# Output weight tiles split at steps 44 to 47, late output banks exchanged, and the last gate products in two parts, in a hybrid decoder layer

## The chip, the cores and the metric

The kernel runs on one core of a Trainium2 chip. The metric is the device time of one execution in microseconds. The core has the engines PE (TensorE, matrix products), DVE (VectorE), ACT (ScalarE), POOL (GpSimd) and SP (SyncE, which issues the transfers). Each works through its own queue in order and waits on semaphores for the others.

## The reference, cut to what matters

One layer on 1024 tokens of width 1024, in float32. A combined projection feeds two mixers: dilated sliding-window attention (8 heads of 64, three patterns) and a gated linear recurrence (4 heads of 128). Their outputs, put side by side, go through one output product, and a squared-relu feed-forward layer follows.

```python
proj = h @ w_in[layer]
q_a, k_a, v_a, q_h, f_h, i_h, g_h = jnp.split(proj, splits, axis=-1)
attn = dilated_mixture_attention(q_a..., k_a..., v_a..., slopes)
attn = rmsnorm(attn.reshape(B, S, ATTN_WIDTH), attn_out_norm[layer])
rec = hgrn2_recurrence(q_h, f_h, i_h, g_h, lower_bounds[layer], hgrn_out_norm[layer])
mixed = jnp.concatenate([attn, rec], axis=-1) @ w_out[layer]
x = x + rmsnorm(mixed, mix_post_norm[layer])
h = rmsnorm(x, mlp_pre_norm[layer])
ff = jnp.square(jax.nn.relu(h @ w_ff1[layer])) @ w_ff2[layer]
x = x + rmsnorm(ff, mlp_post_norm[layer])
```

## The kernel before

Each operand of a product is split into a high and a low part, and a product is three passes on PE (`three_pass`, L88 to L91: high·high, low·high, high·low). One such triple on a 128x512 tile is called a **unit** here. A weight tile is loaded into one of two raw buffers (`raw`, by SP), then `w_split` makes its high part on ACT (L85) and its low part on DVE (L86), and then issues the load of the next tile in the stream; since there are two raw buffers, a load waits until the tile two places ahead has been split. `w_get(i, 0)` splits up to and including tile i. The eight tiles of the output weight are `WO0` to `WO0 + 7` (here tile 0 to tile 7), and `WO_TAG` names where their two parts go: `None` is the common pool (`wh`, `wl`), and a pair of letters names kinds of slabs (then the tiles are called `woh`, `wol`).

Order is written out by hand: nothing reorders the instructions of an engine. After the recurrence heads (`hgrn_core`) come 64 attention steps, `s = 8 * head + i`, where `i` runs over `ITEMS`: D0 to D3 (near blocks), F0 and F1 (far keys), N0 and N1. In each step one item's scores are raised (an exponential on ACT, L886), transposed on PE (`turn`, tiles pt_D, pt_F, pt_N) and split to pth/ptl, ptFh/ptFl or ptNh/ptNl; items of the step before are weighed (`weigh`, tiles pov and pov_far), and scores of later items are looked at (`look`, tiles ps_D, ps_F, ps_N; their reads with the bias go to pd, pf, pn on DVE, L836). Between these PE is given units of other work from `queue`: `UNITS` says how many in each step, half of them before `weigh` and half at the step's end, and `fill` takes one. Until step 47 the units are projections of the next head pairs (`attn_proj`: aq, av, ak, whose results are qf, vf, kf); at step 47 the rest of them is drained, `values_turn` transposes the last value half vf (tile pvt), and from then on the units are those of `early_out`: for tokens 0 to 511 the half of the output product that takes the recurrence outputs (tiles 0 to 3, bank pwe, result esum on ACT, L1092). `row_turn(t, 0)` transposes those recurrence rows (pmt) and splits them into emt.

`hooks` names what else is done at a step between its two halves of units: splits of output weight tiles, loads, norms and transposes of mixed rows. After step 63 the output products are finished with tiles 4 to 7 (`late_out`, bank pwo). Accumulators are four kinds of banks, two of each: mm, s, t and pv. The feed-forward product follows.

Tile 0 is split in before by `values(1)` of the last pair (its unit 4, at about step 44); tiles 1 to 3 and 4 to 6 by hooks, tile 7 behind the last step.

Of the kernel before, what the change touches and what calls it, by code (L numbers as in the profile page):

```python
# [11 lines left out]
AF = mybir.ActivationFunctionType  # L12
ALU = mybir.AluOpType
# [24 lines left out]
def hymba_layer(ctx, tc, x, w_in, w_out, w_ff1, w_ff2, g_pre, lb_logits, g_mix, g_post,  # L38
                g_mlp, g_mlp_post, bias_tab, level_masks, ident_in, fold_in, out):
    nc = tc.nc  # L40
# [112 lines left out]
    for i in range(4 * HH, 4 * HH + 3 * (AH // 2)):  # L153
        stream.append((w_in[i], None))
    WO0 = len(stream)
    WO_TAG = (None, None, ("S", "S"), ("S", "BT"), ("S", "S"), ("S", "T"), ("T", "T"), ("T", "T"))

    def wo_dest(k, tags):
        return lambda: (slab(tags[0], f"woh{k}", F32R), slab(tags[1], f"wol{k}", F32R))
# [12 lines left out]
    def fill(ns, least=False):  # L172
        debt[0] += ns
        if least:
            debt[0] = max(debt[0], 1.0)
        while debt[0] > 0 and queue:
            try:
                cost = next(queue[0])
            except StopIteration:
                queue.pop(0)  # L180
                continue
            if cost is None:
                break
            debt[0] -= cost
        debt[0] = min(debt[0], 0.0)
# [267 lines left out]
    def hgrn_core(h, scale, after=None):  # L453
# [150 lines left out]
        if after is not None:  # L604
            after()
        fill(1500 * scale)
        if h == HH - 1:
            look(0, "N", 0)
        for n in range(NT):
            V.scalar_tensor_tensor(gate[:, n], pos[n // 4][:, n % 4], rs[:, n:n + 1], gate[:, n],  # L610
                                   op0=ALU.mult, op1=ALU.mult)
        nc.sync.dma_start(out=mix_dram[:, h * P:(h + 1) * P].rearrange("(n p) d -> p n d", p=P), in_=gate)


    halves = ((0, 64), (64, 128))
# [106 lines left out]
    def attn_proj(pr):  # L722
        stacks = [{}, {}]
        box = [None]
        while pr > 1 and not second_done[pr - 2]:
            yield None
        w = w_get(A0 + 3 * pr, 0)
        for hf in range(2):
            sl = slice(hf * 512, hf * 512 + 512)
            for n, cost in enumerate(proj_t(w, f"aq{pr}", hf, box)):  # L730
                if hf == 0 and n == 2 and turn_later:
                    values_turn()
                    cost += 450.0
                if hf == 0 and n == 4:
                    w_get(A0 + 3 * pr)
                yield cost
            if hf == 0:
                for i in range(2):
                    stacks[i]["q"] = slab("S", f"q{pr}_{i}", F32R)
            full = half(f"qf{pr}{hf}")  # L740
            V.scalar_tensor_tensor(full, box[0], 0.125, rrow[:, sl], op0=ALU.mult, op1=ALU.mult)
            lo = half(f"ql{pr}{hf}", F32R)
            for i, (a, b) in enumerate(halves):
                S.activation(stacks[i]["q"][a:b, sl], full[a:b], AF.Copy)  # L744
                G.tensor_tensor(out=lo[a:b], in0=full[a:b], in1=f32(stacks[i]["q"][a:b, sl]), op=ALU.subtract)  # L745
            nc.sync.dma_start(out=f32(stacks[0]["q"][64:128, sl]), in_=f32(lo[0:64]))
            nc.sync.dma_start(out=f32(stacks[1]["q"][0:64, sl]), in_=f32(lo[64:128]))
            yield 650.0
        wv = w_get(A0 + 3 * pr + 1, 0)
        vs = None  # L750

        def values(hf):
            for n, cost in enumerate(proj_t(wv, f"av{pr}", hf, box)):
                if n == 4:
                    w_get(A0 + 3 * pr + 1 + hf)
                yield cost
            full = half(f"vf{pr}{hf}")
            V.tensor_tensor(out=by_class(full), in0=in_blocks(box[0]),
                            in1=in_blocks(rrow[:, hf * 512:hf * 512 + 512]), op=ALU.mult)
            turn_later.append((pr, vs, full, hf))  # L760
            yield 650.0

        vs = slab("V8", f"v{pr}", F32R, (P, NT, 2, 2, 64))
        yield from values(0)
        while pr > 0 and not first_done[pr - 1]:
            yield None
        wk = w_get(A0 + 3 * pr + 2, 0)
        for i in range(2):
            stacks[i]["kh"] = slab("S", f"kh{pr}_{i}", F32R)
            stacks[i]["kl"] = slab("S", f"kl{pr}_{i}", F32R)  # L770
        pairs[pr] = (stacks, vs)
        for hf in range(2):
            for n, cost in enumerate(proj_t(wk, f"ak{pr}", hf, box)):
                if n == 2 and hf == 0:
                    values_turn()
                    cost += 450.0
                yield cost
            keys_read(pr, box[0], hf)
            if hf == 0 and pr == AH // 2 - 1:
                early_rows()  # L780
            yield 650.0
        yield from values(1)
# [244 lines left out]
    def row_rec(t):  # L1027
        gain = gains["early"] if t < NE else gains["gmix"][:, :AW]
        G.tensor_tensor(out=rec_row(t), in0=rec_row(t), in1=gain, op=ALU.mult)

    def row_fin(t):
        return anats[-1][:, t].rearrange("p i d -> p (i d)")

    def row_norm(t):
        row = rows[t]
        dump = half(f"dm{t}")
        ss = col("ass", 2)
        sa = col("asa")
        ra = scales["row", t] = tp.tile([P, 1], F32, tag="era", name=f"era{t}") if t < NE else col("ara")
        S.activation(dump[:, :AL], row[:, AW:AW + AL], AF.Square, accum_out=ss[:, 0:1])  # L1040
        S.activation(dump[:, AL:AW], row_fin(t), AF.Square, accum_out=ss[:, 1:2])
        G.tensor_tensor(out=sa, in0=ss[:, 0:1], in1=ss[:, 1:2], op=ALU.add)
        rsqrt_mean(ra, sa, AW, 1)

# [151 lines left out]
    for h in range(HH):  # L1196
        last = h == HH - 1
        queue += [attn_proj(0), attn_proj(1)] if last else [hgrn_ig(h + 1), hgrn_qf(h + 1)]
        if last:
            S.activation(col("texp"), nhalf[:, :1], AF.Exp)  # L1200
        hgrn_core(h, 1.15 if last else 1.0, open_attention if last else None)
        if not last:
            drain()

    hooks = {
        45: lambda: row_rec(0),
        46: lambda: row_rec(1),
        47: lambda: row_turn(0, 0, tag="mm"),
        48: lambda: w_get(WO0 + 1, 0),
        49: lambda: [w_get(WO0 + 2, 0), load_bias(AH - 1), row_rec(2)],  # L1210
        50: lambda: [row_turn(1, 0), row_rec(3)],
        51: lambda: w_get(WO0 + 3, 0),
        52: lambda: [row_turn(2, 0), load_gain("gmix", "R", g_mix)],
        55: lambda: [row_load(t) for t in range(3)],
        59: lambda: [row_norm(0), row_gain(0)],
        60: lambda: [row_norm(1), row_gain(1)],
        61: lambda: [row_turn(0, 1, tag="s"), w_get(WO0 + 4, 0)],
        62: lambda: w_get(WO0 + 5, 0),
        63: lambda: w_get(WO0 + 6, 0),
    }  # L1220
    UNITS = ((2, 3, 3, 4, 3, 3, 3, 3), (3, 3, 3, 4, 2, 3, 3, 2), (3, 3, 3, 4, 2, 3, 3, 2), (2,) * 8)
    ITEMS = (("D", 0), ("D", 1), ("D", 2), ("D", 3), ("F", 0), ("F", 1), ("N", 0), ("N", 1))
    LOOKS = {0: ((0, "D", 2), (0, "N", 1)), 1: ((0, "D", 3), (0, "F", 0)), 2: ((0, "F", 1),),
             6: ((1, "D", 0),), 7: ((1, "D", 1),)}
# [3 lines left out]
    for s in range(n_steps):  # L1228
# [20 lines left out]
            far_queries(hd)  # L1249
        if kind != "D" or g % 2:  # L1250
            to_weigh.append((hd, kind, g // 2 if kind == "D" else g))
        units = UNITS[s // 16][i]
        for _ in range(units // 2):
            fill(0.0, True)
        to_fold, last_fold = [(*w, r) for w in ready for r in [weigh(*w)] if r is not None], to_fold
# [23 lines left out]
            swap_max(hd, int(i == 3))  # L1279
        if i == 7:  # L1280
            look(hd + 1, "N", 0)
        if s == 54:
            row_turn(3, 0, tag="s")
    for *w, r in to_fold:
        finish(*w, *r)
# [905 lines left out]
```

## Time and profile before

| | before |
|---|---|
| median of 3 runs | 1228.99 us (1228.61 to 1230.24) |
| profiled execution | 1228.77 us |
| its span in the trace | 1226.8 us |
| mean granted clock of PE | 0.993 |
| busy: PE, DVE, ACT, POOL | 98%, 71%, 45%, 26% |

In the listings of single instructions each row has its start, its duration, the engine, the line, the operation, the tile written and the tiles read, and the shapes; a bracket at the end gives the idle time of the engine just before it and what ended that. Attention runs from about 304 to 534 us of the span.

### The profile page before, as it was taken

How to read it: one execution, taken by the hardware profiler on the slowest of the kernel's cores; microseconds unless marked ns; L12 is line 12 of the kernel's file. 1: busy time of each engine (PE TensorE's matmuls, PEld its weight loads, DVE VectorE, ACT ScalarE, POOL GpSimd, SP SyncE). 2: the span in 40 equal slices, each digit the busy share in tenths (PEclk: the TensorE clock that was granted, in tenths of full speed). 3: DMA queues.
4: the chain of work that ended last, by engine and by line, in shares of the span. 5: the costliest groups of instructions: out<-in, count | busy, mean ns of one | idle time of the engine just before them, and what ended most of it. 6: DMA issues, size and time to landing. Idle time of an engine off the chain costs nothing.

```text
span 1226.8 us, 17215 instructions
## 1 busy us (share of the span) xinstructions
PE 1205.5 (98%) x6350; PEld 1032.1 (84%) x6350; DVE 868.7 (71%) x1478; ACT 547.4 (45%) x1067; POOL 322.8 (26%) x321
## 2 busy tenths in 40 slices
PE   9999999999999997999999999999999999999998
PEld 8898989888888886878888888888888888888886
DVE  5697979787676666568679667676678555488796
ACT  7633333222665665665575122222244354534562
POOL 0110111012222222145250676756622000000022
PEclk9999999999999998899999999999999999999999
DMA  5231413123453636163324446554487634433337
GB/s 216 70 91 57 120 57 107 35 81 99 120 130 91 162 101 165 54 208 134 135 106 161 167 170 223 202 183 155 156 317 270 234 103 155 154 103 88 118 103 274
DMA packets 86483, 174.21 MB, mean 142 GB/s; under 512 B 12160, under 2 KB 38784, under 8 KB 86400
## 3 DMA queue, kind: packets, MB, share of 16 engines
q1 hardware_dynamic: 86400, 173.12, 43.2%
q8 instruction: 50, 0.82, 0.3%
q14 instruction: 33, 0.27, 0.1%
HBM read 117.76 MB, written 49.04 MB: 136 GB/s over the span
## 4 chain that ended last, share of the span: by engine, by line
PE 94%; DVE 2%; ACT 2%; issue 1%; DMA 1%; SPq 0%; POOL 0%; DVEq 0%; POOLq 0%; ACTq 0%
PE f L1931 18%; PE f2s L1931 7%; PE pig L91 2%; PE pig L89 2%; PE pig L90 2%; PE pl L480 2%; PE pwo L89 2%; PE pwo L91 2%; PE pwo L90 2%; PE pm_f L89 1%; PE pm_f L91 1%; PE pm_f L90 1%; PE pm_ak L89 1%; PE pm_aq L89 1%; PE pm_aq L91 1%; PE pm_aq L90 1%
## 5 line engine op out<-in xcount | busy, mean ns | idle before, releaser
L86 DVE TENSOR_TENSOR al<-ar,ah 128x1024 fp32r<-128x1024 f32 x56 | 70.6, 1261 | 80.1 <-ACT ah L85 77.8
L1931 PE MATMUL f<-bh,ah 128*128 128x512 f32 x320 | 124.5, 389 | 0.0
L1931 PE MATMUL f<-bl,ah 128*128 128x512 f32 x320 | 124.5, 389 | 0.0
L1931 PE MATMUL f<-bh,al 128*128 128x512 f32 x320 | 124.5, 389 | 0.0
L85 ACT ACTIVATE ah<-ar 128x1024 fp32r<-128x1024 f32 x56 | 59.1, 1055 | 86.5 <-DMA ar<-actd 86.1
L1931 PEld LDWEIGHTS f<-bh,ah 128*128 128x128 f32 x320 | 60.1, 188 | 12.6
L1931 PEld LDWEIGHTS f<-bh,al 128*128 128x128 f32 x320 | 60.1, 188 | 12.5
L1931 PEld LDWEIGHTS f<-bl,ah 128*128 128x128 f32 x320 | 60.1, 188 | 12.3
L2005 POOL TENSOR_SCALAR lbl<-ssq 128x1 f32<-128x1 f32 x4 | 3.3, 821 | 245.6 <-ACT fd L2001 245.4
L1554 POOL TENSOR_TENSOR e<-x,e 128x512 f32<-128x512 f32 x14 | 21.6, 1541 | 131.1 <-DVE x L1505 123.9
L1931 PE MATMUL f2s<-bl,ah 128*128 128x512 f32 (+1 forms) x128 | 48.9, 382 | 0.0
L1931 PE MATMUL f2s<-bh,al 128*128 128x512 f32 (+1 forms) x128 | 48.9, 382 | 0.0
L1931 PE MATMUL f2s<-bh,ah 128*128 128x512 f32 (+1 forms) x128 | 48.9, 382 | 0.0
L985 POOL TENSOR_TENSOR anat<-anat,stat 128x128 f32<-128x128 f32 (+1 forms) x24 | 12.2, 509 | 115.8 <-DVE anat L984 105.2
L86 DVE TENSOR_TENSOR bl<-br,bh 128x1024 fp32r<-128x1024 f32 x32 | 40.1, 1253 | 1.2 <-ACT bh L85 1.1
L665 POOL COPY tout<-traw 128x256 f32<-128x256 f32 x16 | 11.9, 745 | 107.1 <-DMA traw<-in_bias_tab_dram 76.4
L1948 ACT ACTIVATE acc<-f 128x512 f32<-128x512 f32 x28 | 16.8, 598 | 49.7 <-PE f L1931 49.7
L86 DVE TENSOR_TENSOR wl<-raw,wh 128x1024 fp32r<-128x1024 f32 x23 | 30.0, 1306 | 10.7 <-ACT wh L85 10.7
L85 ACT ACTIVATE bh<-br 128x1024 fp32r<-128x1024 f32 x32 | 33.6, 1050 | 4.3 <-PE f L1931 2.9
L89 PE MATMUL pwo<-woh,mt 128*128 128x512 f32 x80 | 31.6, 395 | 1.3 <-ACT esum L1092 1.3
L701 POOL TENSOR_TENSOR kl<-kf,kh 64x512 fp32r<-64x512 f32 x16 | 22.2, 1390 | 39.7 <-ACT kh L700 37.4
L745 POOL TENSOR_TENSOR ql<-qf,q 64x512 fp32r<-64x512 f32 x16 | 21.4, 1338 | 42.3 <-ACT q L744 41.7
(1702 smaller groups left out, 4034.7 us busy)
## 6 DMA issues: line engine op xcount, KB each, us to landing
ar<-actd SPq DMA_DIRECT2D x56, 512.0 KB, 3.6
br<-in_w_ff_dram SPq DMA_DIRECT2D x16, 1024.0 KB, 6.2
w1r<-in_w_ff_dram SPq DMA_DIRECT2D x14, 1024.0 KB, 6.4
raw<-in_w_in_dram SPq DMA_DIRECT2D x26, 512.0 KB, 3.8
actd<-e SPq DMA_DIRECT2D x17, 768.0 KB, 4.3
actd<-e SPq DMA_DIRECT2D x11, 1024.0 KB, 4.1
vd<-v SPq DMA_DIRECT2D x16, 256.0 KB, 3.8
raw<-in_w_out_dram SPq DMA_DIRECT2D x8, 512.0 KB, 3.7
```

The lines of the kernel that those rows point to most:

```text
L85: S.activation(hi, src, AF.Copy)
L86: eng.tensor_tensor(out=lo, in0=src, in1=f32(hi), op=ALU.subtract)
L89: TE.matmul(dst, lhs[0], rhs[0], start=start, stop=False)
L90: TE.matmul(dst, lhs[0], rhs[1], start=False, stop=False)
L91: TE.matmul(dst, lhs[1], rhs[0], start=False, stop=stop)
L480: TE.matmul(pl[:, n % 2, :192], kt[:, n * P:(n + 1) * P], sets[u // 2][:, n % 4], start=True, stop=True)
L701: G.tensor_tensor(out=kl[a:b], in0=src, in1=f32(kh[a:b]), op=ALU.subtract)
L745: G.tensor_tensor(out=lo[a:b], in0=full[a:b], in1=f32(stacks[i]["q"][a:b, sl]), op=ALU.subtract)
L985: G.tensor_tensor(out=dst, in0=dst, in1=st["rd"][:, b].unsqueeze(2).to_broadcast([P, n, 64]), op=ALU.mult)
L1554: eng[0].tensor_tensor(out=e1[:, 3], in0=a21, in1=e1[:, 2], op=ALU.add)
L1931: TE.matmul(pm, a[:, j, c], b[:, j, d], start=start and j == 0 and q == 0, stop=stop and j == 1 and q == 2, skip_group_check=True)
L1948: S.activation(acc_at(p, i), pm, AF.Copy)
```

## The change

1. Tile 0 is split by the hook of step 44, tile 1 at 45 (it was 48), tile 2 at 46 (49), tile 3 at 47 (51), and tile 4 at 58 (61); tiles 5 to 7 stay. The places of tiles 1, 2 and 3 are exchanged.
2. Row products, row transposes, bias and row loads around these hooks move by one to four steps; `row_turn(0, 0)` uses a bank t in place of mm. `row_norm` is cut into two parts.
3. `late_out` takes a bank mm for odd and s for even row tiles (it was the other way round).
4. The last head's eight gate products, with the transfer that follows, leave `hgrn_core` and stand in the hooks of steps 0 and 1, four in each.
5. `values_turn` stands one unit later in aq and ak.
6. `UNITS` has a row for each head in place of one for two; heads 4 and 5 get one and three units fewer, head 6 one more, head 7 two fewer. What is left is drained where the queue was drained before. The number of instructions on each engine is the same.

```diff
-    WO_TAG = (None, None, ("S", "S"), ("S", "BT"), ("S", "S"), ("S", "T"), ("T", "T"), ("T", "T"))
+    WO_TAG = (None, ("S", "S"), ("S", "BT"), None, ("S", "S"), ("S", "T"), ("T", "T"), ("T", "T"))
...
+        def gated(g4):
+            for n in range(g4 * 4, g4 * 4 + 4):
+                V.scalar_tensor_tensor(gate[:, n], pos[g4][:, n % 4], rs[:, n:n + 1], gate[:, n],
+                                       op0=ALU.mult, op1=ALU.mult)
+            if g4 == 1:
+                nc.sync.dma_start(out=mix_dram[:, h * P:(h + 1) * P].rearrange("(n p) d -> p n d", p=P), in_=gate)
         if h == HH - 1:
             look(0, "N", 0)
-        for n in range(NT):
-            V.scalar_tensor_tensor(gate[:, n], pos[n // 4][:, n % 4], rs[:, n:n + 1], gate[:, n],
-                                   op0=ALU.mult, op1=ALU.mult)
-        nc.sync.dma_start(out=mix_dram[:, h * P:(h + 1) * P].rearrange("(n p) d -> p n d", p=P), in_=gate)
+            return gated
+        for g4 in range(2):
+            gated(g4)
...
-                if hf == 0 and n == 2 and turn_later:
+                if hf == 0 and n == 3 and turn_later:
                     values_turn()
...
-                if n == 2 and hf == 0:
+                if n == 3 and hf == 0:
                     values_turn()
...
-    def row_norm(t):
+    def row_norm(t, which=(0, 1)):
...
-        pm = pmo[t, hf] = bank("s" if t % 2 else "mm", f"pwo{t}_{hf}")
+        pm = pmo[t, hf] = bank("mm" if t % 2 else "s", f"pwo{t}_{hf}")
...
     hooks = {
-        45: lambda: row_rec(0),
-        46: lambda: row_rec(1),
-        47: lambda: row_turn(0, 0, tag="mm"),
-        48: lambda: w_get(WO0 + 1, 0),
-        49: lambda: [w_get(WO0 + 2, 0), load_bias(AH - 1), row_rec(2)],
-        50: lambda: [row_turn(1, 0), row_rec(3)],
-        51: lambda: w_get(WO0 + 3, 0),
-        52: lambda: [row_turn(2, 0), load_gain("gmix", "R", g_mix)],
-        55: lambda: [row_load(t) for t in range(3)],
-        59: lambda: [row_norm(0), row_gain(0)],
-        60: lambda: [row_norm(1), row_gain(1)],
-        61: lambda: [row_turn(0, 1, tag="s"), w_get(WO0 + 4, 0)],
+        0: lambda: last_gate(0),
+        1: lambda: last_gate(1),
+        43: lambda: row_rec(0),
+        44: lambda: [row_rec(1), w_get(WO0, 0)],
+        45: lambda: w_get(WO0 + 1, 0),
+        46: lambda: [row_turn(0, 0), w_get(WO0 + 2, 0)],
+        47: lambda: [w_get(WO0 + 3, 0), row_rec(2)],
+        49: lambda: [row_turn(1, 0), load_bias(AH - 1), row_rec(3)],
+        51: lambda: row_turn(2, 0),
+        52: lambda: load_gain("gmix", "R", g_mix),
+        55: lambda: [row_load(t) for t in range(2)],
+        57: lambda: [row_norm(t, (0,)) for t in range(2)],
+        58: lambda: w_get(WO0 + 4, 0),
+        59: lambda: [row_norm(0, (1,)), row_gain(0), row_load(2)],
+        60: lambda: [row_norm(1, (1,)), row_gain(1)],
+        61: lambda: row_turn(0, 1, tag="t"),
         62: lambda: w_get(WO0 + 5, 0),
         63: lambda: w_get(WO0 + 6, 0),
     }
-    UNITS = ((2, 3, 3, 4, 3, 3, 3, 3), (3, 3, 3, 4, 2, 3, 3, 2), (3, 3, 3, 4, 2, 3, 3, 2), (2,) * 8)
+    UNITS = ((2, 3, 3, 4, 3, 3, 3, 3), (2, 3, 3, 4, 3, 3, 3, 3), (3, 3, 3, 4, 2, 3, 3, 2), (3, 3, 3, 4, 2, 3, 3, 2),
+             (3, 3, 3, 3, 2, 3, 3, 2), (3, 3, 3, 3, 2, 2, 2, 2), (3, 2, 2, 3, 2, 2, 2, 1), (2, 2, 2, 3, 1, 2, 2, 1))
...
-        units = UNITS[s // 16][i]
+        units = UNITS[hd][i]
...
-        if s == 54:
+        if s == 53:
             row_turn(3, 0, tag="s")
```

How instructions stand on an engine then is shown at three places (line, operation, tile written, tiles read; numbers tell buffers apart). DVE around steps 44 to 47 in before, from the split of F0's far weights to those of N0; `vf` is the last value half, `ISA` the read of scores with the bias:

```order
L921 TENSOR_TENSOR ptFl_4927<-pt_F_4961,ptFh_4926 128x256
L923 TENSOR_TENSOR ptFh_4926<-pt_F_4961,ptFh_4926 64x128 x2
L984 TENSOR_REDUCE anat_4591<-pov_1_4947 128x2x64
L758 TENSOR_TENSOR vf_4991<-pm_av_4899,rrow 128x512
L836 ISA pd_4995,stat_4994<-ps_D_4997,bt_4683 128x128
L836 ISA stat_4994 128x1
L839 TENSOR_SCALAR stat_4994<-stat_4994 128x1
L926 TENSOR_TENSOR ptNl_5004<-pt_N_5002,ptNh_5003 128x4x128
```

The same stretch of DVE in after; `wol` and `emt` are low parts of tiles 1 and 2 and of the first recurrence rows:

```order
L927 TENSOR_TENSOR ptFl_4922<-pt_F_4957,ptFh_4921 128x256
L929 TENSOR_TENSOR ptFh_4921<-pt_F_4957,ptFh_4921 64x128 x2
L990 TENSOR_REDUCE anat_4588<-pov_1_4936 128x2x64
L86 TENSOR_TENSOR wol_4984<-raw_4624,woh_4983 128x1024
L842 ISA pd_4994,stat_4993<-ps_D_4996,bt_4680 128x128
L842 ISA stat_4993 128x1
L845 TENSOR_SCALAR stat_4993<-stat_4993 128x1
L932 TENSOR_TENSOR ptNl_5003<-pt_N_5001,ptNh_5002 128x4x128
L86 TENSOR_TENSOR emt_4794<-pmt_0_5025,emt_4794 128x512
L86 TENSOR_TENSOR wol_5033<-raw_4951,woh_5032 128x1024
L764 TENSOR_TENSOR vf_5041<-pm_av_4908,rrow 128x512
```

Two low halves of weight tiles and the one of emt have come ahead of `vf`.

ACT in before from the last key copy `kh_1` to the first hooks of step 48, where `wh_5115` is tile 1 and `v` the copy of pvt:

```order
L700 ACTIVATE kh_1_4673<-kf_4885 64x4x128
L886 ACTIVATE pd_4995,stat_4994<-pd_4995,stat_4994 128x128
L925 ACTIVATE ptNh_5003<-pt_N_5030 128x4x128
L713 ACTIVATE v_4568<-pvt_5041 128x8x64
L85 ACTIVATE emt_4778<-pmt_0_5062 128x512
L886 ACTIVATE pf_4996,stat_4994<-pf_4996,stat_4994 128x256
L925 ACTIVATE pth_0_5089<-pt_D_5088 128x128
L845 ACTIVATE qc_5094<-q_0_4431 128x512
L966 ACTIVATE pn_4749<-pov_far 128x512
L85 ACTIVATE wh_5115<-raw_4606 128x1024
```

ACT in after from the second copy of N0 to the split of tile 3 (`wh_5081`); `woh_5032` is tile 2:

```order
L931 ACTIVATE ptNh_5002<-pt_N_5001 128x4x128
L892 ACTIVATE pn_4746,stat_4682<-pn_4746,stat_4682 128x256
L706 ACTIVATE kh_1_4673<-kf_4897 64x4x128
L85 ACTIVATE emt_4794<-pmt_0_5025 128x512
L85 ACTIVATE woh_5032<-raw_4951 128x1024
L892 ACTIVATE pd_4994,stat_4993<-pd_4994,stat_4993 128x128
L931 ACTIVATE ptNh_5002<-pt_N_5049 128x4x128
L719 ACTIVATE v_4568<-pvt_5060 128x8x64
L85 ACTIVATE wh_5081<-raw_4987 128x1024
```

The copy of emt and the split of tile 2 now stand ahead of the last ptNh and of `v`, and that of tile 3 ahead of the next raise.

PE in before at the end of attention, from the units around the last transposes pt_N (step 63):

```order
L905 MATMUL pt_N_5645<-ident,pn_5375 128x128 x4
L89 MATMUL pwe_1_5567<-woh_5155,emt_4779 128x512
L90 MATMUL pwe_1_5567<-wol_5156,emt_4779 128x512
L91 MATMUL pwe_1_5567<-woh_5155,emt_4779 128x512
L960 MATMUL pov_far<-ptNh_5617,v_4568 128x4x32
L960 MATMUL pov_far<-ptNl_5618,v_4568 128x4x32
L960 MATMUL pov_far<-ptNh_5617,v_4568 128x4x64
L960 MATMUL pov_far<-ptNl_5618,v_4568 128x4x64
L89 MATMUL pwe_0_5566<-woh_5220,emt_4779 128x512
L90 MATMUL pwe_0_5566<-wol_5221,emt_4779 128x512
L91 MATMUL pwe_0_5566<-woh_5220,emt_4779 128x512
L89 MATMUL pwe_1_5567<-woh_5220,emt_4779 128x512
```

PE in after at the same place:

```order
L89 MATMUL pwe_1_5521<-wh_5081,emt_4795 128x512
L90 MATMUL pwe_1_5521<-wl_5082,emt_4795 128x512
L91 MATMUL pwe_1_5521<-wh_5081,emt_4795 128x512
L911 MATMUL pt_N_5658<-ident,pn_5385 128x128 x4
L966 MATMUL pov_far<-ptNh_5628,v_4568 128x4x32
L966 MATMUL pov_far<-ptNl_5629,v_4568 128x4x32
L966 MATMUL pov_far<-ptNh_5628,v_4568 128x4x64
L966 MATMUL pov_far<-ptNl_5629,v_4568 128x4x64
```

The units that stood between the last pt_N and pov_far, and among the parts of pov_far, are gone from there: they come earlier.

More of the change, by code (lines that the diff above doesn't have):

```diff
@@ L1032, in row_fin @@
         return anats[-1][:, t].rearrange("p i d -> p (i d)")
-    def row_norm(t):
+    def row_norm(t, which=(0, 1)):
         row = rows[t]
-        dump = half(f"dm{t}")
-        ss = col("ass", 2)
+        if 0 in which:
+            ss = scales["part", t] = col("ass", 2)
+            S.activation(half(f"dm{t}")[:, :AL], row[:, AW:AW + AL], AF.Square, accum_out=ss[:, 0:1])
+        if 1 not in which:
+            return
+        ss = scales.pop(("part", t))
         sa = col("asa")
         ra = scales["row", t] = tp.tile([P, 1], F32, tag="era", name=f"era{t}") if t < NE else col("ara")
-        S.activation(dump[:, :AL], row[:, AW:AW + AL], AF.Square, accum_out=ss[:, 0:1])
-        S.activation(dump[:, AL:AW], row_fin(t), AF.Square, accum_out=ss[:, 1:2])
+        S.activation(half(f"dn{t}")[:, AL:AW], row_fin(t), AF.Square, accum_out=ss[:, 1:2])
         G.tensor_tensor(out=sa, in0=ss[:, 0:1], in1=ss[:, 1:2], op=ALU.add)
@@ L1200, in hymba_layer @@
             S.activation(col("texp"), nhalf[:, :1], AF.Exp)
-        hgrn_core(h, 1.15 if last else 1.0, open_attention if last else None)
+        last_gate = hgrn_core(h, 1.15 if last else 1.0, open_attention if last else None)
         if not last:
```

## The prediction

> **What bounds the kernel now.** I read the page first, then what PE (TensorE) waits for, then stretches of the span, then single instructions.
>
> ```profile
> PE 1205.5 (98%) x6350; PEld 1032.1 (84%) x6350; DVE 868.7 (71%) x1478; ACT 547.4 (45%) x1067; POOL 322.8 (26%) x321
> PE 94%; DVE 2%; ACT 2%; issue 1%; DMA 1%; SPq 0%; POOL 0%; DVEq 0%; POOLq 0%; ACTq 0%
> ```
>
> PE is busy for 98% of the span and carries 94% of the chain that ended last. So only two things can move the time: gaps in PE's work, and PE running slow. All PE waits from the attention part on (engine, tile, line, what it waited for: us in total, times, longest):
>
> ```profile
> PE pwe L89 <- ACT woh L85: 3.3, 1, 3.3
> PE pwe L90 <- DVE wol L86: 2.2, 2, 1.6
> ...
> PE pwo L89 <- ACT esum L1092: 1.3, 1, 1.3
> PE pwe L89 <- ACT wh L85: 1.2, 1, 1.2
> PE ps_D L831 <- DVE stat L836: 1.1, 1, 1.1
> PE pwe L89 <- DVE v L714: 1.1, 1, 1.1
> PE pwe L90 <- DVE wl L86: 0.8, 1, 0.8
> ...
> PE pov_far L960 <- DVE ptNl L926: 0.6, 1, 0.6
> ...
> PE pvt L710 <- DVE vf L758: 0.4, 1, 0.4
> PE pt_F L908 <- ACT pf L886: 0.4, 1, 0.4
> PE pt_N L905 <- ACT pn L886: 0.3, 1, 0.3
> PE pwe L89 <- ACT esum L1092: 0.2, 1, 0.2
> ```
>
> The two at the beginning of attention, ps_D and pvt, are 1.5 us. The six of pwe and pov_far that name v, ptNl, wh, wl, woh and wol lie around steps 47 to 50: the early output products start there and their weight tiles are not split yet. The four that remain (pwo, pt_F, pt_N, and pwe for esum) are 2.2 us at the end of attention. By stretches (us, busy of PE, PEld, DVE, ACT, POOL, granted clock, DMA share, GB/s):
>
> ```profile
> 466.00:498.00 32.00, 22.99 (x109) 19.14 (x108) 17.18 (x53) 15.84 (x38) 7.29 (x7) 0.79 0.59 168
> 498.00:530.00 32.00, 31.20 (x200) 27.00 (x199) 19.80 (x64) 23.71 (x70) 6.51 (x14) 1.00 0.11 30
> 470.00:476.00 6.00, 4.08 (x25) 3.30 (x25) 3.90 (x14) 3.43 (x6) 0.00 (x0) 1.00 0.77 178
> 476.00:480.00 4.00, 4.00 (x18) 3.53 (x16) 1.97 (x10) 2.03 (x4) 0.00 (x0) 0.59 0.75 229
> 480.00:484.00 4.00, 2.38 (x14) 1.85 (x14) 2.49 (x7) 0.11 (x1) 3.08 (x3) 0.93 0.72 210
> 484.00:490.00 6.00, 3.54 (x17) 3.08 (x15) 2.44 (x8) 3.00 (x9) 0.92 (x1) 0.75 0.65 206
> 490.00:497.00 7.00, 5.61 (x19) 4.63 (x19) 3.16 (x9) 3.75 (x10) 0.40 (x1) 0.53 0.44 150
> ```
>
> From 466 to 498 PE is idle for 32.00 − 22.99 = 9.0 us, and its clock is 0.79; in the next 32 us the clock is 1.00. All idle that matters: 1.5 + 9.0 + 2.2 = 12.7 us. The clock costs more on top: 4 × 0.41 + 4 × 0.07 + 6 × 0.25 + 7 × 0.47 = 6.7 us, of which 0.47 × (7.00 − 5.61) = 0.6 fell on idle, so 6.1. Single instructions show both (start, us, and in brackets the idle before it):
>
> ```profile
> 475.60 0.49 PE L90 MATMUL pwe<-wl,emt 128*128 128x512 f32 x1 [0.75 <-DVE wl L86]
> 482.02 0.50 PE L90 MATMUL pwe<-wol,emt 128*128 128x512 f32 x1 [1.61 <-DVE wol L86]
> 490.84 0.79 PE L89 MATMUL pwe<-woh,emt 128*128 128x512 f32 x1 [3.29 <-ACT woh L85]
> 494.02 0.78 PE L89 MATMUL pwe<-woh,emt 128*128 128x512 f32 x1
> 495.45 0.41 PE L942 MATMUL pov<-pth,v 128*128 128x256 f32 x1
> 529.26 0.39 PE L89 MATMUL pwe<-woh,emt 128*128 128x512 f32 x1
> 529.96 0.39 PE L89 MATMUL pwe<-woh,emt 128*128 128x512 f32 x1
> ```
>
> A product of three passes (a unit) takes 529.96 − 529.26 = 0.70 us at full clock and 495.45 − 494.02 = 1.43 us behind the stalls. Before loses 12.7 + 6.1 = 18.8 us that the change could reach.
>
> **The change part by part.** The rows that carry prices:
>
> ```profile
> 307.04 2.15 DVE L610 SCALAR_TENSOR_TENSOR gate<-po,hrs,gate 128x128 f32<-128x128 f32 x8
> 309.11 0.54 DVE L836 CUSTOM_DVE_ANT_0 pd<-ps_D,bt 128x384 f32<-128x384 f32 x1
> 464.66 1.10 DVE L758 TENSOR_TENSOR vf<-pm_av,rrow 128x512 f32<-128x512 f32 x1
> 467.27 0.60 PE L710 MATMUL pvt<-ident,vf 128*128 128x128 f32 x4
> 462.76 0.35 SPq L106 DMA_DIRECT2D raw<-in_w_out_dram  x1
> 473.24 1.05 ACT L85 ACTIVATE wh<-raw 128x1024 fp32r<-128x1024 f32 x1
> 474.32 1.22 DVE L86 TENSOR_TENSOR wl<-raw,wh 128x1024 fp32r<-128x1024 f32 x1
> 528.62 0.59 ACT L925 ACTIVATE ptNh<-pt_N 128x512 fp32r<-128x512 f32 x1
> 530.00 0.33 SPq L106 DMA_DIRECT2D raw<-in_w_out_dram  x1
> 533.60 1.07 ACT L85 ACTIVATE woh<-raw 128x1024 fp32r<-128x1024 f32 x1
> 534.71 1.22 DVE L86 TENSOR_TENSOR wol<-raw,woh 128x1024 fp32r<-128x1024 f32 x1 [1.19 <-ACT woh L85]
> 536.10 0.40 PE L90 MATMUL pwo<-wol,mt 128*128 128x512 f32 x1
> ```
>
> *Last gate products in two parts.* Eight products hold DVE for 2.15 us ahead of the score read pd at 309.11, for which ps_D waits 1.1. In hooks 0 and 1 four (1.07) stand behind that read, where PE has units to do. The 1.1 goes; pvt, one unit (0.70) later, loses its 0.4. Gain 1.5; if the halves delayed a later read it would be 0.4. The mixd transfer goes out a step later; SP's order is unchanged and the early rows are read 40 steps on.
>
> *Weight splits at steps 44 to 47.* These take away the late tiles: the waits for wh, wl, woh and wol, the one for v (pmt now takes a bank t, so pwe need not wait until pvt was read) and with them most of 9.0 us. What is late next is read off the queues. On DVE, vf (the last value tile, from which pvt is made) now stands behind wol of tile 2. That tile's load can go out only when tile 0's low half has freed its buffer: 462.76 before, up to 0.7 earlier now, since the new table puts two units fewer ahead of step 44. A load takes 533.60 − 530.00 = 3.6, so the tile is there at 465.7 to 466.4. Then 1.05 on ACT, 1.22 on DVE, and 1.10 of vf: it ends at 469.1 to 469.8, in place of 465.8. PE comes to pvt at 466.7 (467.27 less the wait of 0.6) to 467.3. The new wait of pvt is therefore 1.8 to 3.1 us; I take 2.65, since ACT has an emt copy just ahead. Behind it DVE splits tile 3 ahead of the reads of pn: of its 1.22 I leave 0.75 as a wait of ps_N, the rest lying beside PE's pwe unit, and 0.25 for pt_N at steps 46 and 47, behind two ACT splits. Sum 3.65 (2 to 6), in place of 9.0.
>
> *Tile 4 at step 58.* Its low half (1.22 on DVE) stands ahead of the joint maximum of the far scores, and the raise and pt_F follow from that. Before, pt_F waited 0.4 there with no split. Below: 0.4, all hidden. Above: 1.05 + 1.22 = 2.3. I take 1.45 as the whole loss there, nearer to the DVE price.
>
> *The end.* The pwo bank exchange takes away the wait for esum, 1.3. But the last tile's chain stays: its load goes out at 530.00 when tile 5's low half is done, and runs through ACT (533.60) and DVE (534.71) to the product at 536.10, 6.1 us. Before, PE did 6.1 − 1.3 = 4.8 of work meanwhile. The new table moves three units (2.1) from there to earlier steps, and with tile 4's split (1.05 on ACT) gone from step 61 the chain can start that much sooner: 4.8 − 2.1 + 1.05 = 3.75 of work, 2.35 lost; 3.4 if ACT is no earlier. Where PE meets it: no unit stands between the last pt_N and its pov_far now, where three stood, so it waits for ptNh (0.59 on ACT, behind other ACT work; I take 1.05) and ptNl (0.75), and the last 1.45 for tile 7. I take the sum of these, 3.25 (2.35, or up to 4.15 where ptNl's wait comes on top of 3.4), nearer to the case without a sooner ACT, since the raises of N1 still stand there. It takes the place of 1.8 (pwo, pt_N, esum); pt_F's 0.4 is counted above.
>
> *At nothing.* Units moved between steps are the same count at 0.70; PE has as many instructions as before. The row products, norms and loads that move stand on POOL (26% busy by the page) and on ACT beside units. Without that cover a norm part, an ACT pass over at most 384 columns, would cost no more than ptNh's 0.59. The slabs exchanged hold tiles that are free by then. FF1's first bank now follows tile 7's pwo; a clash there would cost one DVE read of a bank, some 1.1 by the row of vf.
>
> *The clock.* Stalls after: 3.65 + 1.45 + 3.25 = 8.35. Is PE slowed again? In before, 1.2 + 0.8 of idle close together at 474 to 476 preceded 476:480 at 0.59, and the 1.3 at the end preceded nothing. The pvt wait of 2.65 is nearer to the first, so one such stretch, 4 × 0.41 = 1.6, and 0.4 for a second at the end: 2.0 (0 to 6.1). The Trainium skill, "TensorE: Matmul & The Clock Gate", section "Part 1: The HAM clock gate (the "warmup" mystery)", has half speed only after an idle window of about 3.4 us. The trace does not agree: 0.59 came with no single idle over 1.2. By that rule this term would be 0.
>
> Sum: losses 8.35 + 2.0 = 10.35 in place of 18.8, a gain of 8.45. Against the profiled execution's own 1228.77 us (span 1226.8 and 2.0 around it) that gives 1220.3. The median of the runs is 1228.99, 0.2 away, which I neglect.
>
> **The rivals.**
> *A, the backlog hides.* ACT and DVE catch up beside the units; losses of the three places fall to their lower ends, 2 + 0.4 + 2.35 = 4.75, no slow stretch. Gain 14.05: 1214.7. For it: DVE is idle for over 14 of the 32 us from 466. Against: the load of tile 2 can't be there earlier.
> *B, stalls as forecast but no slow stretch.* Gain 18.8 − 8.35 = 10.45: 1218.3. For it: the pwo wait of 1.3 left the clock at 1.00. Against: 476:480.
> *C, stalls as forecast and the clock drops as long as before.* Losses 8.35 + 6.1 = 14.45, gain 4.35: 1224.4. For it: three stalls over 1.5 us would do what 482.02 and 490.84 did.
> *D, slower: the softmax falls behind ACT.* Three splits at steps 45 to 47 stand ahead of raises and copies on ACT and of reads on DVE. Should each of steps 47 to 50 wait out one split of both, 1.05 + 1.22 = 2.27, that adds 9.1; with a clock loss of 6.1 the losses are 8.35 + 9.1 + 6.1 = 23.6, 4.8 more than before: 1233.6. It decides once losses pass 18.8, that is, from about two such steps with the full clock loss. Against: from 498 to 530 ACT is 23.71 of 32 busy and PE waited for next to nothing.
>
> **How the numbers follow.** A measurement of this kernel can tell about 0.2%, 2.5 us, from no change. Forecast 0.37, A 0.20, B 0.12, C 0.16, losses within 2.5 us of before's 0.05, D 0.10. Faster: 0.37 + 0.20 + 0.12 + 0.16 = 0.85; same 0.05; slower 0.10. The range reaches from 1213, where A's first place loses next to nothing too, to 1227, C with the upper ends of all three places (6 + 2.3 + 4.15 = 12.45 + 6.1 = 18.55 would be 1228.5; I take a good half of the way there); D and a fifth of A lie outside.
>
> **What would show it.** Right: no wait of pwe for wh, wl, woh or wol; a wait of pvt for vf of 1.8 to 3.1; some 1.4 of pt_F behind step 58; pov_far and pwo waiting for ptNh, ptNl and wol at the end; ps_D's 1.1 gone; one stretch of clock near 0.6. Wrong: pvt without a wait (A), clock below 0.8 over some 30 us (C), or raises late in every step from 47 to 50 (D).

## The result, and the profile after

The changed kernel takes 1220.01 us (median of 4 runs, 1219.55 to 1220.62) beside 1228.82 of the kernel before (4 runs, 1228.61 to 1230.24): a ratio of 0.9926, 95% interval 0.9909 to 0.9943. The profiled execution took 1219.76 us, its span is 1218.0 and the mean granted clock 0.997.

What PE waits for in the whole span of the kernel after:

```profile
PE pvt L716 <- DVE vf L764: 3.0, 1, 3.0
PE pt_F L914 <- ACT pf L892: 1.5, 2, 1.0
...
PE pwo L90 <- DVE wol L86: 0.8, 1, 0.8
PE pt_N L911 <- DVE ptNl L932: 0.7, 1, 0.7
PE pov_far L966 <- ACT ptNh L931: 0.6, 1, 0.6
PE ps_F L837 <- DVE stat L842: 0.6, 1, 0.6
...
PE pov_far L966 <- DVE ptNl L932: 0.5, 1, 0.5
PE pwo L89 <- ACT woh L85: 0.4, 1, 0.4
```

No product of the early output (pwe) waits for a split tile any more. In the place of those waits stands one wait of pvt, 3.0, with pt_N's 0.7 just ahead. The other rows are pt_F (1.5, behind step 58), four at the end (0.6 + 0.5 + 0.4 + 0.8 after rounding, 2.2 by single rows) and a new one, ps_F's 0.6 at step 1. The same 32 us as before, and the two stretches behind the wait of pvt (columns as in the prediction):

```profile
466.00:498.00 32.00, 28.65 (x180) 25.54 (x181) 22.45 (x69) 20.73 (x56) 4.96 (x6) 0.95 0.68 181
```

```profile
470.47:473.10 2.63, 2.63 (x10) 2.34 (x11) 1.73 (x5) 1.48 (x3) 0.00 (x0) 0.50 0.68 211
473.10:476.00 2.90, 2.90 (x21) 2.69 (x21) 2.77 (x10) 2.35 (x7) 0.00 (x0) 0.97 0.65 144
```

PE is idle for 32.00 − 28.65 = 3.4 us instead of 9.0, and the clock is 0.95 instead of 0.79. The clock is 0.50 for 2.63 us and then near full speed: 0.50 × 2.63 + 0.03 × 2.90 = 1.4 us lost in place of 6.1. The wait of pvt and what made it, on PE, DVE, POOL and ACT in turn:

```profile
470.47 1.11 PE L716 MATMUL pvt<-ident,vf 128*128 128x128 f32 x4 [3.04 <-DVE vf L764]
471.23 0.78 PE L89 MATMUL pwe<-wh,emt 128*128 128x512 f32 x1
472.66 0.41 PE L837 MATMUL ps_N<-kh,q 128*128 128x256 f32 x1
```

```profile
460.62 1.84 DVE L86 TENSOR_TENSOR wl<-raw,wh 128x1024 fp32r<-128x1024 f32 x1 [0.87 <-ACT wh L85]
464.04 1.22 DVE L86 TENSOR_TENSOR wol<-raw,woh 128x1024 fp32r<-128x1024 f32 x1
467.35 2.11 DVE L86 TENSOR_TENSOR wol<-raw,woh 128x1024 fp32r<-128x1024 f32 x1 [0.39 <-ACT woh L85]
469.38 1.03 DVE L764 TENSOR_TENSOR vf<-pm_av,rrow 128x512 f32<-128x512 f32 x1
```

```profile
458.83 2.54 POOL L1035 TENSOR_TENSOR erows<-erows,etable 128x512 f32<-128x512 f32 x2
464.08 1.43 POOL L991 TENSOR_TENSOR anat<-anat,stat 128x128 f32<-128x128 f32 x1 [2.71 <-DVE anat L990]
467.11 1.27 POOL L1035 TENSOR_TENSOR erows<-erows,etable 128x512 f32<-128x512 f32 x1
```

```profile
465.63 0.60 ACT L85 ACTIVATE emt<-pmt 128x512 fp32r<-128x512 f32 x1
466.25 1.06 ACT L85 ACTIVATE woh<-raw 128x1024 fp32r<-128x1024 f32 x1
```

vf runs right behind tile 2's low half, as the order said. But that half took 2.11 us where the prediction had 1.22. Tile 0's low half (460.62) was long too, 1.84, beside two POOL products; so it freed tile 2's buffer late, and the load went out at 462.48, 0.3 earlier than before where up to 0.7 was forecast. Behind the wait a unit of pwe takes 472.66 − 471.23 = 1.43 us, half speed, as in the stretches of before.

### The profile page after: what moved, and what is told of

The parts are those of the page before. It is cut to its first block, busy times and chain, and to the rows that moved or that the text cites. A ratio compares the mean times of both kernels' runs of the same rounds, so it can differ in the third digit from the quotient of the medians.

```text
span 1218.0 us, 17222 instructions
## 1 busy us (share of the span) xinstructions
PE 1200.7 (99%) x6350; PEld 1028.1 (84%) x6350; DVE 868.3 (71%) x1478; ACT 546.9 (45%) x1067; POOL 323.4 (27%) x321
## 4 chain that ended last, share of the span: by engine, by line
PE 94%; ACT 2%; DVE 2%; issue 1%; DMA 1%; SPq 0%; POOL 0%; DVEq 0%; POOLq 0%; ACTq 0%
PE f L1945 18%; PE f2s L1945 7%; PE pig L91 2%; PE pig L89 2%; PE pig L90 2%; PE pl L480 2%; PE pwo L90 2%; PE pwo L91 2%; PE pwo L89 2%; PE pm_f L89 1%; PE pm_ak L89 1%; PE pm_f L91 1%; PE pm_f L90 1%; PE pm_ak L91 1%; PE pm_ak L90 1%; PE pm_av L89 1%
```

## The experiments

Each ratio is to the kernel before, run on the same chip (its medians there were 1228.19, 1229.00 and 1228.87 us in the three groups of four); the changed kernel's is 0.9926. The intervals are about ±0.0016, that is ±2 us, and most of that is the spread of the kernel before (4 to 7 us in a group, against 0.6 to 2.7 for most of the others). Two kernels of the lists are therefore compared by their medians: differences under 1 us are not told apart, and between groups the medians of before themselves differ by up to 0.8.

### The early splits undone, and the early splits alone

```diff
-        44: lambda: [row_rec(1), w_get(WO0, 0)],
-        45: lambda: w_get(WO0 + 1, 0),
-        46: lambda: [row_turn(0, 0), w_get(WO0 + 2, 0)],
-        47: lambda: [w_get(WO0 + 3, 0), row_rec(2)],
+        44: lambda: row_rec(1),
+        46: lambda: row_turn(0, 0),
+        47: lambda: row_rec(2),
+        48: lambda: w_get(WO0 + 1, 0),
...
+        49: lambda: [w_get(WO0 + 2, 0), row_turn(1, 0), load_bias(AH - 1), row_rec(3)],
+        51: lambda: [w_get(WO0 + 3, 0), row_turn(2, 0)],
```

(and `WO_TAG` as before.)

> The changed kernel with one part undone: tiles 0 to 3 are split where they were before (tile 0 by the value units, 1 to 3 at steps 48, 49 and 51) and lie where they did. Theory of the prediction: the waits of pwe for split tiles (9.0 us) and the clock loss behind them (6.1) come back, and pvt's wait of 3.0, pt_N's 0.7 and their slow stretch (about 1.1) go, so +10 us: 1230. Rival, that the new table of units and not the earlier split took the waits away: under +4 us, 1220 to 1224.

Measured: 1224.25 us, 0.9963 (0.9949 to 0.9977), 4.2 slower than the changed kernel. The time is far from the theory's 1230 and just above the rival's range, but the rival's reason does not hold either: the waits come back, only smaller than they were.

```profile
PE pwe L90 <- DVE wol L86: 2.0, 2, 1.2
PE pwe L89 <- ACT woh L85: 1.7, 1, 1.7
...
PE pwe L89 <- ACT wh L85: 1.2, 1, 1.2
...
PE pwe L90 <- DVE wl L86: 0.8, 1, 0.8
...
PE pvt L716 <- DVE vf L764: 0.6, 1, 0.6
```

That is 2.0 + 1.7 + 1.2 + 0.8 + 0.6 = 6.3 us in place of 9.0 in before, and the clock from 466 to 498 is 0.89 in place of 0.79. At the end pov_far waits for nothing here, and pwo only 0.3 for wol, though the table of units is the new one.

The other way round, the kernel before with the splits moved and nothing else:

```diff
-        45: lambda: row_rec(0),
-        46: lambda: row_rec(1),
-        47: lambda: row_turn(0, 0, tag="mm"),
-        48: lambda: w_get(WO0 + 1, 0),
+        44: lambda: w_get(WO0, 0),
+        45: lambda: [row_rec(0), w_get(WO0 + 1, 0)],
+        46: lambda: [row_rec(1), w_get(WO0 + 2, 0)],
+        47: lambda: [row_turn(0, 0, tag="mm"), w_get(WO0 + 3, 0)],
```

> The kernel before with one part of the change alone: tiles 0 to 3 split at steps 44 to 47, at their new places; the table of units, the banks, tile 4 and the gate products are as before. Theory: the late tiles' waits and the clock loss behind them go; vf stands ahead of tile 2's low half with the old table, so pvt hardly waits; pwe still waits for v, about 1: 9 to 11 us faster than before, 1217 to 1219. Rival, from the run with late splits, which lost only 4 us: 4 to 5 faster, 1224.

Measured: 1219.65 us, 0.9929 (0.9917 to 0.9942): 9 us, as much as the whole change. Alone, the splits also bring waits with them (the profiled execution took 1221.42 us):

```profile
PE pwe L89 <- DVE v L714: 2.2, 1, 2.2
PE pov_far L960 <- DVE ptNl L926: 1.7, 2, 1.2
...
PE pwo L90 <- DVE wol L86: 0.8, 1, 0.8
```

pwe waits for v 2.2 us here (1.1 in before); pmt still stands in a bank mm, and v's low part comes late behind the splits, but no run parts the two. The end already has the waits of the changed kernel, though the table is the old one: pov_far waits 0.32 for ptNh and 0.50 for ptNl there (the other 1.16 of its 1.7 falls at 468.6), and pwo 0.76 for wol. And pwo does not wait for esum, though the banks are the old ones. So the splits are worth 9 us beside the old table and banks and 4 beside the new ones; the parts do not add up.

### Rows and banks alone, the table of units alone

Only `row_rec(0)`, `row_rec(1)` and `row_turn(0, 0)` moved (43, 44, 46; bank t):

> The kernel before with the first row products at 43 and 44 and the first row transpose at 46 in a bank t, nothing else. Theory: pwe's wait for v of 1.07 and pov_far's 0.56 go, and the tiles are as late as ever: PE meets them earlier, and 0 to 2 us are won, 1226 to 1228. Rival, that this part made the six us by which the run with late splits has less loss in the middle than before: 1222 to 1223.

Measured: 1227.31 us, 0.9989 (0.9980 to 0.9998): 1.4 us faster, as the theory said. v's wait is gone, and woh's is still 3.0.

Only `UNITS` new:

> The kernel before with the new table of units alone. Theory: the table costs where the splits are early, since it pushes vf behind tile 2's low half, but gains where they are late, since fewer units are asked for while the tiles are not split: the waits of pwe fall from 9.0 to about 6.5 and the clock loss with them, 3 to 6 us, 1223 to 1226. Rival, that it costs in both: 1229 to 1231.

Measured: 1227.80 us, 0.9990 (0.9977 to 1.0003): no difference that can be told, so both theories miss. Taken at their middle values, these two parts (1.4 and 1.2, the second not told apart from none) and the gate products (0.9 by their waits) make about 3.5 of the 4.6 us by which the kernel with late splits beats the kernel before. The rest of that is not attributed.

### The table of units undone

```diff
-        units = UNITS[hd][i]
+        units = UNITS[s // 16][i]
```

(with the old table.)

> The changed kernel with the table of units as before. Theory: three units stand at the end of attention again and cover 1.5 of its 2.2 us of waits, the pvt wait stays at about 3: -1 to -1.5 us, 1218.8. Rival, that the earlier splits need the fewer units of heads 4 and 5 ahead of them: the pvt wait grows by up to 1.4 and the time by 1 to 3 us, 1221 to 1223.

Measured: 1216.64 us, 0.9901 (0.9885 to 0.9916): 3.4 faster than the changed kernel, more than expected. Part of it is the end, where pov_far and pwo wait 1.2 in place of 2.2 and pt_F 1.1 in place of 1.5; the larger part is the middle:

```profile
PE pt_N L911 <- DVE ptNl L932: 2.0, 1, 2.0
...
PE pwe L89 <- DVE v L720: 0.7, 1, 0.7
```

```profile
466.00:498.00 32.00, 29.59 (x192) 26.09 (x193) 23.62 (x79) 23.39 (x61) 5.22 (x6) 1.00 0.68 181
```

pvt does not wait, since vf now stands ahead of tile 2's low half; pt_N waits 2.0 in its place, and the clock stays at 1.00. To see which rows of the table do it, those of heads 4 and 5 alone were put back:

```diff
-             (3, 3, 3, 3, 2, 3, 3, 2), (3, 3, 3, 3, 2, 2, 2, 2), (3, 2, 2, 3, 2, 2, 2, 1), (2, 2, 2, 3, 1, 2, 2, 1))
+             (3, 3, 3, 4, 2, 3, 3, 2), (3, 3, 3, 4, 2, 3, 3, 2), (3, 2, 2, 3, 2, 2, 2, 1), (2, 2, 2, 3, 1, 2, 2, 1))
```

> The changed kernel with the rows of heads 4 and 5 of the table as before, those of heads 6 and 7 new. Theory: the units missing ahead of step 44 made the value tile late, so the middle is that of the run with the old table (no wait of pvt over 1, clock 1.00) and the end that of the changed kernel (2.2 of waits): 2 to 2.5 us faster than the changed kernel, 1217.7. Rival, that heads 6 and 7 make the difference: 1219 to 1220.

Measured: 1217.68 us, 0.9902 (0.9884 to 0.9919), the time expected. In its trace the middle is that of the whole old table (pt_N 2.0, no wait of pvt, clock 1.00 from 468 to 476) and the end that of the changed kernel. On DVE, vf stands ahead of tile 2's low half:

```profile
464.70 1.06 DVE L764 TENSOR_TENSOR vf<-pm_av,rrow 128x512 f32<-128x512 f32 x1
467.52 2.13 DVE L86 TENSOR_TENSOR wol<-raw,woh 128x1024 fp32r<-128x1024 f32 x1 [0.16 <-ACT woh L85]
```

So the four units taken from heads 4 and 5 make vf late: the value product ends later against the hooks, which stay at their steps. (Head 7 gets one unit fewer by the new row, 15 in place of 16, not two as the list of the change says.)

### vf ahead of tile 2

```diff
-        46: lambda: [row_turn(0, 0), w_get(WO0 + 2, 0)],
-        47: lambda: [w_get(WO0 + 3, 0), row_rec(2)],
+        46: lambda: row_turn(0, 0),
+        47: lambda: [w_get(WO0 + 2, 0), row_rec(2)],
+        48: lambda: w_get(WO0 + 3, 0),
```

> The changed kernel with tile 2 split by the hook of step 47, behind the value transpose, and tile 3 by that of 48, so that vf no longer stands behind tile 2's low half on DVE. Theory: pvt's wait of 3.04 us goes, and the slow stretch behind it (about 1.3) with it: -3 to -4 us, 1216 to 1217. Rival, that DVE and ACT are simply full there: the wait reappears at pwe for wol or at ps_N, under -1.5 us.

Measured: 1216.04 us, 0.9896 (0.9883 to 0.9910), 4 faster than the changed kernel. The theory holds: pvt's wait falls to 0.58, the clock is 1.00, and no pwe waits for tile 2 or 3 though they are split a step later.

```profile
467.54 0.66 PE L716 MATMUL pvt<-ident,vf 128*128 128x128 f32 x4 [0.58 <-DVE vf L764]
```

```profile
466.00:498.00 32.00, 30.85 (x201) 27.27 (x201) 23.32 (x79) 22.83 (x61) 4.52 (x6) 1.00 0.65 179
```

PE has only 32.00 − 30.85 = 1.2 us of idle left there. A little of the rival shows all the same: ps_N waits 0.6, which it did not in the changed kernel.

### POOL's product moved away from the split

```diff
-        44: lambda: [row_rec(1), w_get(WO0, 0)],
+        44: lambda: [row_rec(1), row_rec(2), w_get(WO0, 0)],
...
-        47: lambda: [w_get(WO0 + 3, 0), row_rec(2)],
+        47: lambda: w_get(WO0 + 3, 0),
```

> The changed kernel with row_rec(2), a POOL product over erows, moved from the hook of step 47 to that of 44. In the changed kernel tile 2's low half took DVE 2.11 us in place of 1.22, while POOL worked on kl and erows. Theory, that POOL's work beside it is the cause: the low half takes 1.22 to 1.6, pvt's wait falls from 3.04 to 2.2 to 2.6, the time by 0.5 to 1.3 us. Rival, that it is the weight load that lands then: 2.11 stays and so does the time.

Measured: 1219.54 us, 0.9925 (0.9911 to 0.9938): the mechanism as expected, the time unchanged within what can be told. Tile 2's low half takes 1.23, and pvt's wait is 1.88, less even than the 2.2 to 2.6 expected. But the moved product now stands in the way of tile 0's low half, which took 1.84 beside two POOL products in the changed kernel and takes 3.08 beside three (DVE, POOL and PE in turn):

```profile
460.18 3.08 DVE L86 TENSOR_TENSOR wl<-raw,wh 128x1024 fp32r<-128x1024 f32 x1 [0.86 <-ACT wh L85]
467.89 1.23 DVE L86 TENSOR_TENSOR wol<-raw,woh 128x1024 fp32r<-128x1024 f32 x1 [0.22 <-ACT woh L85]
```

```profile
459.66 2.53 POOL L1035 TENSOR_TENSOR erows<-erows,etable 128x512 f32<-128x512 f32 x2
```

```profile
463.78 0.33 PE L960 MATMUL pov_far<-ptFl,vf 128*128 128x128 f32 x1 [0.55 <-DVE ptFl L927]
467.13 0.66 PE L911 MATMUL pt_N<-ident,pn 128*128 128x128 f32 x4 [0.97 <-DVE ptNl L932]
470.12 0.66 PE L716 MATMUL pvt<-ident,vf 128*128 128x128 f32 x4 [1.88 <-DVE vf L764]
```

0.55 + 0.97 + 1.88 = 3.4 us of waits stand against 0.70 + 3.04 = 3.7 in the changed kernel, and the clock from 466 to 498 is 0.95 in both.

### Gate products and late banks undone

The gates ahead of step 0 again:

> The changed kernel with the eight last gate products ahead of step 0 again. Theory: ps_D waits 1.1 again and ps_F's new 0.55 goes, pvt's 0.4 stays away: +0.5, 1220.5. Rival, that the wait merely moved to the next score read: 0.0.

Measured: 1220.64 us, 0.9933 (0.9919 to 0.9948). The waits are as expected (ps_D 1.1 back, ps_F's 0.55 gone); 0.6 us is in line with it, though not told apart from none.

The banks of pwo and of `row_turn(0, 1)` as before:

> The changed kernel with the banks of the late output products and of the first late row transpose as before. Theory: the wait for esum of 1.3 comes back, but it lies within the last tile's chain, so that the waits for woh and wol (0.35 and 0.76) shrink by as much as they can: +0.2 to +0.5, about 1220.3. Rival, that the exchange is worth the whole wait: +1.3, 1221.3.

Measured: 1219.89 us, 0.9925 (0.9911 to 0.9940): no difference. Both theories miss: with the old banks, too, the trace has no wait of pwo for esum, as in the run with the splits alone. The other waits at the end are the same to 0.01 us.

### All of it together

Tile 2 at 47 and tile 3 at 48 as above, and:

```diff
-        1: lambda: last_gate(1),
+        2: lambda: last_gate(1),
...
-        58: lambda: w_get(WO0 + 4, 0),
+        56: lambda: w_get(WO0 + 4, 0),
...
-        61: lambda: row_turn(0, 1, tag="t"),
-        62: lambda: w_get(WO0 + 5, 0),
+        61: lambda: [row_turn(0, 1, tag="t"), w_get(WO0 + 5, 0)],
```

> The changed kernel with tile 2 at step 47 and tile 3 at 48 (as in the run with vf first), tile 4 at 56 in place of 58, tile 5 at 61 in place of 62, and the second half of the gate products at step 2 in place of 1. Theory: beside pvt's wait, pt_F's 1.5, ps_F's 0.55 and half of the 2.2 at the end go: 1216.0 less 2 to 3, 1213 to 1214. Rival, that the splits only move on to the next read on DVE: 1215.5 to 1217.

Measured: 1213.19 us, 0.9867 (0.9848 to 0.9886): the theory's time, 6.8 us faster than the changed kernel and 2.9 faster than the run with vf first. pt_F's 1.5 has become 0.4, and no pwo waits. ps_F's wait did not go: one of 0.6 stays at step 1 and one of 0.5 is new at tile 4.

```profile
PE ps_F L837 <- DVE stat L842: 1.1, 2, 0.6
...
PE pt_F L914 <- ACT pf L892: 0.4, 1, 0.4
PE pov_far L966 <- ACT ptNh L931: 0.4, 1, 0.4
PE pov_far L966 <- DVE ptNl L932: 0.3, 1, 0.3
```

```profile
309.10 1.11 DVE L610 SCALAR_TENSOR_TENSOR gate<-po,hrs,gate 128x128 f32<-128x128 f32 x4
310.14 0.67 DVE L842 CUSTOM_DVE_ANT_0 pd<-ps_D,bt 128x512 f32<-128x512 f32 x1
```

It is the first half of the gate products, not the second, that stands ahead of the read of pd there, and the reads of pf that ps_F waits for come right behind that: the second half had moved and the wait is the same.

The same with the old table, and tile 1 at 46:

> As the run before this one, with the old table of units and with tile 1 at step 46 in place of 45. Theory: pt_N's wait of 2.05 in the run with the old table, which stood behind tile 1's and vf's work on DVE, goes too, and the end is covered by more units: 1216.6 less 3 to 4, 1212.5 to 1213.5. Rival: tile 1 is late for its units at pwe, 1.5 of wait, 1215.

Measured: 1213.81 us, 0.9871 (0.9852 to 0.9891). A little above the theory's range and below the rival's 1215: pt_N's 2.0 becomes 0.9, but ps_D waits 1.1 and pwe 0.7 for v, and the clock from 468 to 476 is 0.79. Its time is not told apart from that of the run just above.

## Why the prediction was right

The forecast was 1220.3 with 0.85 for faster; measured 1220.0. The single waits on PE in the changed kernel, from which its losses are summed:

```profile
312.52 0.36 PE L837 MATMUL ps_F<-kh,qc 128*128 128x192 f32 x1 [0.55 <-DVE stat L842]
```

```profile
466.31 0.66 PE L911 MATMUL pt_N<-ident,pn 128*128 128x128 f32 x4 [0.70 <-DVE ptNl L932]
```

```profile
510.14 0.44 PE L914 MATMUL pt_F<-ident,pf 128*128 128x128 f32 x2 [0.59 <-ACT pf L892]
513.46 0.44 PE L914 MATMUL pt_F<-ident,pf 128*128 128x128 f32 x2 [0.95 <-ACT pf L892]
```

```profile
520.74 0.38 PE L966 MATMUL pov_far<-ptNh,v 128*128 128x256 f32 x1 [0.62 <-ACT ptNh L931]
521.62 0.39 PE L966 MATMUL pov_far<-ptNl,v 128*128 128x256 f32 x1 [0.50 <-DVE ptNl L932]
525.76 0.50 PE L89 MATMUL pwo<-woh,mt 128*128 128x512 f32 x1 [0.35 <-ACT woh L85]
527.02 0.51 PE L90 MATMUL pwo<-wol,mt 128*128 128x512 f32 x1 [0.76 <-DVE wol L86]
```

By the prediction's own steps, from the profiled executions (losses in us; pvt's 3.04 is shown above):

| term | forecast | measured |
|---|---|---|
| steps 44 to 48 | 3.65 | 0.70 + 3.04 = 3.7 |
| tile 4 at step 58 | 1.45 | 0.59 + 0.95 = 1.5 |
| the end | 3.25 | 0.62 + 0.50 + 0.35 + 0.76 = 2.2 |
| gate products | 0 | 0.55 |
| clock | 2.0 | 1.4 |
| sum (18.8 in before) | 10.35 | 9.5 |

The gain by this is 18.8 − 9.5 = 9.3; 0.6 of it was given back at the start of the kernel, where the first transposes waited 1.3 for their load instead of 0.7 for a split (the other kernels show anything from none to 1.3 there), so 8.7, against spans that differ by 8.8. The two pages split it in the same way: PE's busy time, in which a slow clock shows, falls from 1205.5 to 1200.7 us, by 4.8 (6.1 − 1.4 = 4.7 by the sums), and its idle time from 21.3 to 17.3, by 4.0.

```profile
PE 1200.7 (99%) x6350; PEld 1028.1 (84%) x6350; DVE 868.3 (71%) x1478; ACT 546.9 (45%) x1067; POOL 323.4 (27%) x321
```

The 6.1 of the prediction leaves out the clock loss on idle time in one of its four stretches only; left out in all four it would be 1.64 + 0.17 + 0.89 + 2.64 = 5.3. With 5.3 the busy time would have fallen by 3.9, so the pages' 4.8 is nearer to the 6.1. Also, the wait of 0.4 for vf that the prediction puts at the beginning of attention stood at 269.8 us, in the last recurrence head; it went as forecast.

That the total came so close is in part luck. The end and the clock were 1.0 and 0.6 too dear in the forecast, and the gate products' 0.55 and the 0.6 at the start of the kernel were not in it. The 3.65 of steps 44 to 48 is made of other terms than forecast, too: pvt waits 3.04 (2.65), pt_N 0.70 (0.25), and ps_N not at all (0.75).

What held: PE alone sets the time, so waits and clock add up; the tiles' waits at pwe go; vf becomes late behind tile 2's low half, and at the place and of the size that the queues gave. Shown by a run: with vf ahead, the 3.0 and the slow stretch go.

Half right: the size of pvt's wait. ACT took the tile at 466.25, right behind the emt copy that the prediction named (465.63 + 0.60) and inside the forecast 465.7 to 466.4, and its part took 1.06 as forecast. The term that failed is the 1.22 of the DVE split: it took 2.11, with a POOL product beside it. So vf ended at 469.38 + 1.03 = 470.4 and not by 469.8. PE came at 467.4, just behind the forecast, and the wait stayed within 1.8 to 3.1. With 1.22 it would have been about 2.15; the 2.65 that was taken covers both by chance. pt_N's wait came from DVE and not from two ACT splits: ptNl began at 465.57, behind the low halves of tiles 0 and 1, 1.1 after ACT had made ptNh (464.47).

What failed in the attribution: "These take away the late tiles [...] and with them most of 9.0 us" is right for the splits alone (9 us), but the new table, whose moves the prediction put "at nothing" but for three units at the end, costs 3.4 us beside them, and it makes the very wait that the prediction found. Its step "Units moved between steps are the same count" overlooked that a unit moved past a hook changes which of two DVE instructions comes first. And "The pwo bank exchange takes away the wait for esum" is not shown: with the old banks that wait is not there either, and with the splits alone, beside the old banks, it is gone as well, so the splits are enough to remove it. "The new table moves three units (2.1) from there to earlier steps" gives the table what is mostly the splits' work: with the splits alone the end waits for ptNh, ptNl and wol as in the changed kernel, and with late splits and the new table it hardly waits. `fill` gives no unit while the tile that it needs is not split, so late splits leave units over for the end. The table's own share there is about 1 us (2.2 against 1.2 with the old one). The end was over-sized by 1.0, nearer to the case of 2.35 in which ACT reaches tile 5 sooner.

Of the rivals, A (1214.7) is what vf first brings close to; D needed raises late at every step from 47 to 50, and no such row is there.

The clock: 3.04 us of wait were followed by 2.6 us at half speed. The Trainium skill's rule, "TensorE: Matmul & The Clock Gate", section "Part 1: The HAM clock gate (the "warmup" mystery)", of an idle window of about 3.4 us, taken as one gap, would have left the clock whole here too; the trace does not agree, as before. Neither does a single length decide: with the old table a wait of 2.05 left it at 1.00, and in the last run above waits of 0.92, 1.07 and 0.66 within 6 us went with 0.79 from 468 to 476. What decides between these stays open.

## What to carry to other kernels

Where one engine is 98% busy and its order is fixed, write its gaps and its slow stretches down as a sum, and price an edit by who stands ahead of the next producer in the other engines' queues: what is late next is read off there. Filler work is not neutral: moved past a hook it reorders the side engines, so undo a table of counts on its own before keeping it. Work that side engines do in advance should stand behind what PE needs next, not ahead of it: here two splits, put a step later, were worth 4 us.

## What the hardware showed that was not expected

In these traces a DVE split and a POOL product that meet do not share, they queue, and the time that one stands behind the other is shown as its own duration, not as idle. The split of 128x1024 takes 1.22 us alone. In the changed kernel it started at 467.35, while a POOL product ran from 467.11 to 467.11 + 1.27 = 468.38, and ended at 469.46, 1.08 behind the product's end. Tile 0's, begun at 460.62 beside POOL products until 458.83 + 2.54 = 461.37, ended 1.09 behind them. With the later product moved it took 1.23, and tile 0's, which then began at 460.18 with POOL products back to back until 459.66 + 2.53 = 462.19, took 3.08 and ended 1.07 behind the last of them; that last one began at 460.90, later than the split, and still went ahead of it. The other way round, a POOL product that began 0.04 behind a split (464.08) took 1.43, where one alone takes 0.40 (this row is of the kernel before):

```profile
458.76 0.40 POOL L985 TENSOR_TENSOR anat<-anat,stat 128x128 f32<-128x128 f32 x1 [2.55 <-DVE anat L984]
```

The Trainium skill says this in "SBUF — State Buffer", section "SBUF: two separate sides": a DVE instruction with two inputs from SBUF and a GpSimd one lock the same pair of ports for the whole instruction, and whoever starts first has it. The traces agree that one waits out the other in the four cases of this section in which they met; that the last product of three went ahead of a split begun before it is not what "first" would give. vf, which reads a bank, took 1.07 beside a POOL product in the run with vf first.
